# Seven products C by B moved to the transposes of B in a two-layer trunk (Mamba-2 layer, then differential attention)

## The chip, the core and the metric

The kernel runs on one core of one Trainium2 chip. The metric is device microseconds of the whole program, the median of three runs. The core has TensorE (the matmul engine, PE in the profile, with its weight loads shown as PEld), VectorE (DVE), ScalarE (ACT), GpSimd (POOL) and SyncE (SP). Each engine works through its own list of instructions in order and waits at semaphores for the others. Matmuls write to PSUM, eight banks of 128x512 float32; everything else lies in SBUF.

## The reference, cut to what matters

One sequence of 512 tokens of width 1024 goes through a Mamba-2 layer and a differential-attention layer. The change touches the state-space part of the first layer alone. It has eight groups; per group there are B and C (512 tokens x 128 states) and four heads of width 64:

```
cb     = einsum("blgn,bsgn->blsg", c_c, b_c)                            # C by B
y_diag = einsum("blsgr,bsgrp->blgrp", cb[..., None] * decay, x_c)
y_off  = einsum("blgn,bgrpn->blgrp", c_c, state) * exp(acs)[..., None]
new_state = state * exp(acs[:, -1])[..., None, None] + einsum("blgn,blgrp->bgrpn", b_c, x_c * to_end[..., None])
y = gated_group_rms_norm(y + d_skip * xs, z, gate_norm_g)
```

Ahead of it stand an RMS norm, the input projection and a causal convolution of four taps with SiLU; behind it the out projection, added to the residual stream. B and C of a group come out of the convolution.

## The kernel before, in words

**Tiling.** Tokens are cut into four chunks of 128. Large products (input projection, out projection, attention projections) are float32 products made of three matmuls on a high and a low part of each operand (`mm3`, L264). Such a triple over 128 inputs and 512 columns is one unit of the dense stream. The weights arrive from HBM and are split into `whi` (ScalarE) and `wlo` (VectorE).

**Order of the dense stream.** `order_a` (L111) is z0 g0 g1 z1 g2 g3 z2 g4 o0 g5 z3 g6 g7 o1 o2 o3: z is a quarter of the gate projection, g a group's projection to B, C and x, o a quarter of the out projection. Each item has 32 units, o3 has 16 here. `first_layer` (L632) counts units from the start of g0 with `n`. Behind the last unit of an item g, the generator `ssd(g)` (L675) of that group starts.

**What lies between the units.** `ssd(g)` is cut by `yield` into pieces, and `PLACES` (L40) says for each piece and each group how many units behind the end of the group's projection it is put. `resume` (L627) keeps a list `due` of (place, length of the list at that moment); `first_layer` sorts it by these two and, at each unit, issues all pieces whose place has come. The pieces are:

- "cb": four products of C by B into the PSUM bank `pcb` (eight matmul records, since a float32 matmul is two);
- "bt": three transposes of B into `pbt`, copied to `bt` by ScalarE;
- "xt": eight transposes of x into `pxt`; VectorE makes `xdt` and `dx` of them (four instructions), GpSimd makes `xe` of `xdt` (three), and VectorE multiplies `dec`, the decays, by `pcb` (four instructions, L711);
- "st": state products `psA`, `psB` (from `bt` and `xe`) and 64 small products `pyd` (from `dec` and `xdt`); VectorE and GpSimd build the states `hst`;
- "o1", "o2": products `po` of C with the states; then VectorE, GpSimd and ScalarE form gate, squares and the root of the group norm (`y_y`, `y_c`), and ScalarE scales four chunks to `tmp`;
- "y0": eight transposes `pyt` of `tmp`, copied and split to `yh`, `yl` for the out projection.

```
        yield "cb"
        pcb = long_bank(f"pcb{g}")
        for c in range(NQ):
            T.matmul(pcb[:, cs], lhsT=bc[:, cs], rhs=cc[:, cs], start=True, stop=True)
        yield "bt"
        pbt = ss_bank(f"pbt{g}")
        for c in range(3):
            T.transpose(pbt[:, c * P:(c + 1) * P], bc[:, c * P:(c + 1) * P], ident)
```

**What sets the order on each engine.** In this stretch TensorE's instructions keep the order of the program (`T.on`, L785). The order on VectorE, ScalarE and GpSimd is chosen when the program is built, by a planner that runs its own timeline: an engine that is free takes, of the instructions that are ready in that timeline, the one written earliest, and weight splits come with high priority. So `dec` by `pcb` is written in piece "xt" but may stand on VectorE well ahead of `xdt`.

**Buffers.** `pcb` and half of `pyd` share the one bank `long`. B after the convolution has one buffer (the convolution of the next group's B waits for the transposes of this one), C has two, `dec` has two.

Of the kernel before, what the change touches and what calls it, by code (L numbers as in the profile page):

```python
# [37 lines left out]


PLACES = {  # L40
    "cb": (10, 2, 14, 14, 5, 5, 14, 12),
    "bt": (10, 29, 21, 47, 35, 25, 23, 37),
    "xt": (18, 37, 31, 52, 43, 36, 31, 43),
    "st": (29, 47, 39, 63, 53, 47, 39, 53),
# [1240 lines left out]
```

## Time and profile before

| what | value |
|---|---|
| median of three runs | 703.73 us (703.64 to 704.46) |
| profiled execution | 705.32 us, of which the span from first to last instruction is 703.5 us |
| mean granted TensorE clock | 0.998 |
| busy: PE, PEld, DVE, ACT, POOL | 695.2, 580.7, 527.0, 426.3, 115.7 us |
| chain that ended last, share by engine | PE 93%, DVE 2%, ACT 1%, DMA 1% |
| products C by B | 64 records, 8.4 us busy, mean 274 ns |

The times of the profile are microseconds from the start of the span. A timeline row gives the start, the time from the first start to the last end of the merged instructions, engine, line, operation, tiles (out<-in), shape, how many, and in brackets the idle time of the engine before it and what ended it. L74 is the line of a helper, so the tiles' names say which instruction a row is. Matmuls overlap: the distance between two starts tells more of TensorE than the length of one.

### The profile page before, as it was taken

The numbers are of one execution on the slowest core, as the hardware profiler recorded it, in microseconds if no ns is written. First come the engines' busy times: TensorE is split into PE (matmuls) and PEld (weight loads), VectorE is DVE, ScalarE is ACT, GpSimd is POOL, SyncE is SP. The second block draws the span as 40 slices with busy tenths as digits, with TensorE's granted clock in tenths as the row PEclk, the third lists the DMA queues.
The fourth block names the chain that finished last, engine by engine and source line by source line (L and its number), as shares of the span: only waits on it lengthen the run. The fifth ranks groups of instructions, "written<-read, shape, count | busy, mean of one in ns | idle before, by whom it ended". The sixth has DMA issues, their size and how long they took to land.

```text
span 703.5 us, 10459 instructions
## 1 busy us (share of the span) xinstructions
PE 695.2 (99%) x3833; PEld 580.7 (83%) x3833; DVE 527.0 (75%) x1190; ACT 426.3 (61%) x928; POOL 115.7 (16%) x154
## 2 busy tenths in 40 slices
PE   9999999999999999999999999999999999999996
PEld 7888888878888888888888888888888888888884
DVE  6789957799489678568995857467778757787876
ACT  7949474474664637537536258567777667665546
POOL 0025332502415035151211101000000000000002
PEclk9999999999999999999999999999999999999999
DMA  9562404215124313313222112413112221130103
GB/s 340 224 267 85 143 38 165 75 61 180 46 84 170 113 68 120 120 61 120 65 87 90 61 60 68 180 60 120 61 61 96 75 69 61 61 117 4 31 1 119
DMA packets 12627, 70.85 MB, mean 101 GB/s; under 512 B 1568, under 2 KB 2592, under 8 KB 5152
## 3 DMA queue, kind: packets, MB, share of 16 engines
q1 hardware_dynamic: 12288, 69.92, 27.6%
q8 instruction: 30, 0.49, 0.3%
q10 hardware_dynamic: 288, 0.26, 0.1%
q14 instruction: 21, 0.17, 0.1%
HBM read 68.02 MB, written 2.16 MB: 100 GB/s over the span
## 4 chain that ended last, share of the span: by engine, by line
PE 93%; DVE 2%; ACT 1%; issue 1%; DMA 1%; POOL 0%; ACTq 0%; POOLq 0%; SPq 0%
PE pg L74 21%; PE po L74 16%; PE pz L74 13%; PE pt L74 8%; PE pq L74 6%; PE pk L74 6%; PE pv L74 6%; PE pb L74 3%; PE sc L74 3%; PE pyd L74 2%; PE pc L74 2%; PE pyt L74 1%; PE pxt L74 1%; PE psA L74 1%; DMA dec<-acs_d 1%
## 5 line engine op out<-in xcount | busy, mean ns | idle before, releaser
L74 DVE SCALAR_TENSOR_TENSOR wlo<-raw,prm,whi 128x512 fp32r<-128x512 f32 (+1 forms) x236 | 146.8, 674 | 46.9 <-ACT whi L74 46.7
L74 ACT ACTIVATE whi<-raw,prm 128x512 fp32r<-128x512 f32 (+1 forms) x236 | 130.5, 629 | 34.1 <-PE pg L74 8.2
L74 PE MATMUL pg<-a_hi,whi 128*128 128x512 f32 x256 | 102.5, 400 | 0.0
L74 PE MATMUL pg<-a_hi,wlo 128*128 128x512 f32 x256 | 99.9, 390 | 0.0
L74 PE MATMUL pg<-a_lo,whi 128*128 128x512 f32 x256 | 99.7, 390 | 0.0
L74 DVE SCALAR_TENSOR_TENSOR xc<-pg,prc,xc 128x511 f32<-128x511 f32 (+2 forms) x96 | 71.0, 746 | 11.6 <-ACT xc L74 10.4
L74 PEld LDWEIGHTS pg<-a_hi,wlo 128*128 128x128 f32 x256 | 48.1, 188 | 10.2
L74 PEld LDWEIGHTS pg<-a_hi,whi 128*128 128x128 f32 x256 | 48.1, 188 | 9.6
L74 PEld LDWEIGHTS pg<-a_lo,whi 128*128 128x128 f32 x256 | 48.1, 188 | 9.4
L74 PE MATMUL po<-whi,yh 128*128 128x512 f32 x128 | 51.2, 400 | 0.0
L74 PE MATMUL pz<-whi,a_hi 128*128 128x512 f32 (+1 forms) x130 | 49.9, 400 | 0.0
L74 PE MATMUL po<-whi,yl 128*128 128x512 f32 x128 | 49.9, 390 | 0.0
L74 PE MATMUL po<-wlo,yh 128*128 128x512 f32 x128 | 49.9, 389 | 0.0
L74 PE MATMUL pz<-wlo,a_hi 128*128 128x512 f32 (+1 forms) x130 | 48.8, 391 | 0.0
L74 PE MATMUL pz<-whi,a_lo 128*128 128x512 f32 (+1 forms) x130 | 48.7, 390 | 0.0
L1084 POOL TENSOR_TENSOR ot<-x_tok,fg 128x512 f32<-128x512 f32 x4 | 5.0, 1288 | 246.9 <-DVE x_tok L74 246.9
L74 ACT ACTIVATE xc<-xc 128x512 f32<-128x512 f32 x32 | 20.3, 633 | 38.4 <-DVE xc L74 34.5
L74 DVE CUSTOM_DVE_ANT_0 s<-sc,bias 128x128 f32<-128x128 f32 (+3 forms) x64 | 29.4, 488 | 15.9 <-PE sc L74 15.4
L74 ACT ACTIVATE s<-s,mx 128x128 f32<-128x128 f32 (+3 forms) x64 | 35.7, 559 | 9.0 <-DVE mx L74 8.9
L74 ACT ACTIVATE xc<-pg,prc 128x512 f32<-128x512 f32 x32 | 24.8, 776 | 26.5 <-DVE pg L74 25.5
L74 ACT ACTIVATE tmp<-dx 128x256 f32<-128x256 f32 x32 | 13.2, 413 | 45.5 <-DVE dx L74 45.5
L708 POOL TENSOR_TENSOR xe<-xdt,tok 128x256 f32<-128x256 f32 x24 | 14.1, 615 | 162.0 <-DVE xdt L74 162.0
(252 smaller groups left out, 1659.4 us busy)
## 6 DMA issues: line engine op xcount, KB each, us to landing
raw<-in_w_in SPq DMA_DIRECT2D x22, 1024.0 KB, 4.8
raw<-in_w_kvqg SPq DMA_DIRECT2D x16, 1024.0 KB, 4.8
dec<-acs_d SPq DMA_DIRECT2D x8, 1024.0 KB, 5.0
raw<-in_w_out SPq DMA_DIRECT2D x8, 1024.0 KB, 4.8
raw<-in_w_bo SPq DMA_DIRECT2D x4, 1024.0 KB, 4.8
x_tok<-in_x SPq DMA_DIRECT2D x4, 512.0 KB, 9.2
head<-in_first SPq DMA_DIRECT2D x3, 512.0 KB, 6.0
out<-ot SPq DMA_DIRECT2D x6, 256.0 KB, 2.1
```

The source lines that it names most:

```text
L74: i = op(*args, **kw)
L708: GP.tensor_tensor(out=xe[:, c], in0=xdt[:, c], in1=toe_tok[:, c, hs].unsqueeze(2).to_broadcast([P, R, HD]), op=ALU.mult)
L1084: GP.tensor_tensor(out=o, in0=y, in1=f, op=ALU.mult)
```

## The change

Row "cb" of `PLACES` gets the values of row "bt". Nothing else is edited.

```diff
 PLACES = {
-    "cb": (10, 2, 14, 14, 5, 5, 14, 12),
+    "cb": (10, 29, 21, 47, 35, 25, 23, 37),
     "bt": (10, 29, 21, 47, 35, 25, 23, 37),
```

Group 0 keeps its place. For the others, worked out from `order_a`, the places and the sorting of `due`, counted in units from the start of g0:

| group | "cb" before | "cb" after | order on TensorE at the new place |
|---|---|---|---|
| 1 | 66, between o1 and o2 of group 0 | 93 | products, transposes of B |
| 2 | 142 | 149 | y0 of group 1, products, transposes of B |
| 3 | 174, ahead of o1 and o2 of group 2 | 207 | products, y0 of group 2, transposes of B |
| 4 | 229, behind o2 of group 3 | 259 | products, y0 of group 3, transposes of B |
| 5 | 293 | 313 | y0 of group 4, products, transposes of B |
| 6 | 366 | 375 | y0 of group 5, products, transposes of B |
| 7 | 396 | 421 | products, y0 of group 6, transposes of B |

At three of the seven places y0 of the group before comes between the products and the transposes, because a piece that is put on the list anew stands behind one of the same place and number that is there already. At group 2, 5 and 6 y0 is ahead of both.

## Rows read from the trace of the kernel before

**Rows 1.** Page, part 1: busy us, share of the span, records

```profile
PE 695.2 (99%) x3833; PEld 580.7 (83%) x3833; DVE 527.0 (75%) x1190; ACT 426.3 (61%) x928; POOL 115.7 (16%) x154
```

**Rows 2.** Waits of TensorE, whole span: us in total, times, longest

```profile
PE warm L74 <- DVE blank L74: 1.5, 1, 1.5
```

**Rows 3.** Timeline of TensorE at the products of groups 0 and 2

```profile
59.21 1.05 PE L74 MATMUL pcb<-xc,xc 128*128 128x128 f32 x8
60.10 0.49 PE L74 MATMUL pbt<-ident,xc 128*128 128x128 f32 x3
...
142.15 1.05 PE L74 MATMUL pcb<-xc,xc 128*128 128x128 f32 x8
142.95 0.48 PE L74 MATMUL pg<-a_hi,whi 128*128 128x512 f32 x1
143.27 0.40 PE L74 MATMUL pg<-a_lo,whi 128*128 128x512 f32 x1
```

**Rows 4.** Timeline of TensorE at y0 of groups 1 and 5

```profile
147.59 0.39 PE L74 MATMUL pg<-a_hi,wlo 128*128 128x512 f32 x1
148.04 1.96 PE L74 MATMUL pyt<-ident,tmp 128*128 128x128 f32 x8
149.84 0.49 PE L74 MATMUL pbt<-ident,xc 128*128 128x128 f32 x3
...
150.41 0.40 PE L74 MATMUL pg<-a_lo,whi 128*128 128x512 f32 x1
150.64 0.40 PE L74 MATMUL pg<-a_hi,wlo 128*128 128x512 f32 x1
...
334.32 1.03 PE L74 MATMUL pyt<-ident,tmp 128*128 128x128 f32 x8
```

**Rows 5.** Timeline of ScalarE at the scaling of groups 1 and 5

```profile
147.50 1.69 ACT L74 ACTIVATE tmp<-dx,y_y 128x256 f32<-128x256 f32 x4
...
330.99 1.70 ACT L74 ACTIVATE tmp<-dx,y_y 128x256 f32<-128x256 f32 x4
```

**Rows 6.** Timeline of VectorE at the end of group 1's root

```profile
146.78 0.15 DVE L74 SCALAR_TENSOR_TENSOR y_y<-y_c,y_y 128x4 f32<-128x4 f32 x1
146.85 2.47 DVE L74 TENSOR_TENSOR dec<-dec,pcb 128x512 f32<-128x512 f32 x4
```

**Rows 7.** Windows from transposes of B to pyd: length, busy by engine (records), clock, DMA

```profile
149.80:164.20 14.40, 14.40 (x71) 12.10 (x70) 13.48 (x22) 10.43 (x17) 1.76 (x3) 1.00 0.20 74
...
196.30:210.70 14.40, 14.40 (x74) 11.99 (x72) 12.19 (x19) 7.71 (x13) 1.76 (x3) 1.00 0.22 76
...
335.20:348.70 13.50, 13.50 (x67) 11.11 (x65) 12.79 (x20) 9.85 (x17) 1.76 (x3) 1.00 0.22 79
```

**Rows 8.** Timeline of VectorE in group 6, up to xdt

```profile
334.28 2.32 DVE L74 SCALAR_TENSOR_TENSOR xc<-pg,prc,xc 128x511 f32<-128x511 f32 x3 [0.85 <-ACT xc L74]
...
337.83 0.69 DVE L74 TENSOR_TENSOR yl<-pyt,yh 128x512 fp32r<-128x512 f32 x1 [0.64 <-ACT yh L74]
...
343.86 0.69 DVE L74 TENSOR_TENSOR xdt<-pxt,tok 128x512 f32<-128x512 f32 x1
```

**Rows 9.** Timeline of GpSimd at xe of groups 2 and 6

```profile
161.39 1.76 POOL L708 TENSOR_TENSOR xe<-xdt,tok 128x256 f32<-128x256 f32 x3 [24.32 <-DVE xdt L74]
...
345.83 1.76 POOL L708 TENSOR_TENSOR xe<-xdt,tok 128x256 f32<-128x256 f32 x3 [26.03 <-DVE xdt L74]
```

**Rows 10.** Timeline of TensorE at the state products of groups 2 and 6

```profile
163.36 1.02 PE L74 MATMUL psA<-xe,bt 128*128 128x256 f32 x4
...
347.33 1.02 PE L74 MATMUL psA<-xe,bt 128*128 128x256 f32 x4
348.19 0.59 PE L74 MATMUL psB<-xe,bt 128*128 128x256 f32 x2
```

**Rows 11.** Timeline of VectorE at the last state of group 6

```profile
355.51 0.42 DVE L74 TENSOR_TENSOR hst<-psB,hst 128x256 f32<-128x256 f32 x1
```

**Rows 12.** Timeline of TensorE at o1 and o2 of group 6

```profile
356.53 1.46 PE L74 MATMUL po<-hst,xc 128*128 128x256 f32 x6
```

## The prediction, made before the changed kernel was run

> **What bounds the kernel now.** I read the page first, then the waits of TensorE, then the timeline of TensorE around every product C by B and every place that it moves to, and last the lists of ScalarE, VectorE and GpSimd there. The first thing to see is that TensorE is busy for 99% of the span, and that no engine comes near it: VectorE has 75%, ScalarE 61% [rows 1]. The waits name only 1.5 us for TensorE, at the very start [rows 2]. So an instruction that is moved along TensorE's list neither adds nor takes away work; time can change only where TensorE, in its own order, reaches something before its operands are there.
>
> The list of waits does not show all such places, because a wait of TensorE inside a run of transposes is counted as busy. Look at y0 of group 1: eight transposes take 1.96 us, while the same eight take 1.03 in group 5, and they begin 0.45 us behind the start of the dense matmul ahead of them, where two dense matmuls are 0.23 apart [rows 4]. That is 0.93 + 0.22 = 1.15 us of waiting. What they wait for stands on ScalarE: four scalings from 147.50 to 149.19, 0.49 each and 0.40 from one to the next, so the first ends at 147.99 and the first transpose starts at 148.04 [rows 4, 5]. It is the one place between the setup and the last items where I found TensorE over 0.3 us late, and the change touches it.
>
> **The products themselves.** Eight records take from 142.15 to 142.95, 0.80 us, and the dense matmul behind them is followed by the next one after 0.32 instead of 0.23 us [rows 3], so a set of products costs 0.80 + 0.09 = 0.89 us of TensorE. Does it become cheaper next to other float32 work? In group 0 products and transposes stand side by side already, and there the step from the first to the second is 0.89, not 0.80 [rows 3]: the 0.09 is paid between them too. Bounds: nothing saved, and 7 x 0.09 = 0.6 saved if each set lost its changeover; I take 0, by the row of group 0, which is this very pair.
>
> The Trainium skill, "TensorE: Matmul & The Clock Gate", section "Back-to-back issue gap", gives about 81 ns for a matmul of 128 columns in a stream of loads and matmuls. Eight would be 0.65 us, and the sum below would be +1.3 instead of +1.5; the row has 100 ns for each, and the row decides.
>
> **Part 1: y0 of group 1 is reached earlier and waits longer.** Before, the products of group 2 stand at 142.15, ahead of y0; after, they stand behind it. TensorE then comes to y0 0.89 us sooner. Does what it waits for come sooner too? The scalings follow the last step of the root on VectorE, which begins at 146.78; the four products of `dec` by `pcb` stand behind that step, at 146.85 [rows 6], so taking them from this spot frees nothing that the root needs. The root follows the sums of squares and, through them, GpSimd's and VectorE's work on group 1, none of which reads the moved products. So the wait grows from 1.15 by 0.89, and the products are then paid behind it: +0.89 us. Bounds: 0, if the scalings come 0.89 sooner, and 1.5, if the planner puts one 0.69 us product more between two steps of the root (0.60 from start to start, a quarter of 2.40 from rows 6). I take +0.9.
>
> The other six y0: at groups 3, 4 and 7 the products are put ahead of y0 of the group before, so TensorE reaches it no more than 0.4 us sooner (where the transposes of B changed sides with it). At groups 5 and 6 it is reached 0.89 sooner. In group 5's y0, the tighter of the two, the last scaling ends at 332.69 and the first transpose that needs it, three steps of 0.11 behind 334.32, starts at 334.65: 1.96 of slack, 1.07 after [rows 4, 5]. Price 0; without that slack each would cost up to 0.89.
>
> **Part 2: VectorE's four products come later.** They are 2.47 us in one piece, 2.40 as an addition to a full list [rows 6], once per group. Before, they fall soon behind the products, far ahead of `pyd`, which reads them. After, they are not ready before the transposes of B and must be done by `pyd`. What VectorE has free between these two is the question. Group 2 has 14.40 - 13.48 = 0.92, group 3 has 2.21, group 6 has 13.50 - 12.79 = 0.71 [rows 7]. The four groups not shown have more than group 3 and hide the four products, as group 3 does but for 0.2; the cover is this idle time, and if it were gone each would pay as group 6 does.
>
> What stands behind them in the two full stretches is `xdt`, then GpSimd's `xe`, then TensorE's `psA` and `psB`. In group 6 `xdt` starts at 343.86 with no idle time before it, the three `xe` (0.61 apart) end at 346.44, 347.01 and 347.59, and `psA` and `psB` want them at 347.33, 347.76 and 348.19 [rows 8 to 10]. The least slack is 0.60.
>
> How far does `xdt` slip? VectorE has 2.40 us more to do. It gets some back: the convolution products at 334.28 waited 0.85 for ScalarE [rows 8], and ScalarE was free for that at 332.69, when its scalings end [rows 5], so with VectorE's old slot empty they start about 0.85 sooner. The second idle time, 0.64 at 337.83 [rows 8], may be filled too. Slip: 2.40 - 0.85 - 0.64 = 0.9 with both, 1.55 with the first alone. Less the slack: a stall of 0.3 or of 0.95. Below both stands 0, if the planner puts the four products behind `xdt` (they then end near 347.2, ahead of `pyd`, which follows `psB`). Above them 2.40 - 0.60 = 1.8, if nothing is won back. I take 0.6, between the two middle values.
>
> In group 2 the least slack is at `psB` as well: the third `xe` ends at 163.15, and `psB` starts 0.86 behind `psA`'s 163.36, as in group 6, so 1.07 [rows 9, 10]. TensorE comes 0.89 later there, by part 1, so 1.96 against a slip of 2.40 less what is won back: 0. Bound above: 0.4.
>
> The next thing behind is o2 of group 6, whose last pair of matmuls starts 0.86 behind 356.53 and needs a state that VectorE ends at 355.93: slack 1.46 [rows 11, 12]. With the products of group 7 gone from ahead of it, it is reached 0.89 sooner, slack 0.57, and any stall at `psA` widens that again. Price 0; up to 1.2 if VectorE is the full 1.8 behind.
>
> **Sum.** +0.9 + 0.6 = +1.5 us on the profiled execution, 705.32 (span 703.5 and 1.8 around it), so 706.8 there. The median of the three runs shown is 1.59 below that execution; carried over, 703.73 + 1.5 = 705.2.
>
> **Rivals.**
>
> *Part 1 alone.* The planner puts the four products of group 6 behind `xdt`, or wins back more than I think. For it: they are written behind `xdt`. Against: before, the planner let them start ahead of it in every group. +0.9, 704.6.
>
> *VectorE pays in full.* The four products go ahead of `xdt`, nothing is won back, and the root of group 1 gets one more product between its steps: 0.9 + 0.6 + 1.8 = +3.3, 707.0. For it: VectorE's list in group 6 has 0.71 us free [rows 7], and a delay there has no gap to vanish in. Against: the slot that becomes empty is just ahead.
>
> *Not slower: the root of group 1 is planned tighter.* Three products of the next convolution, 2.3 us for such three [rows 8], stand between the last steps of that root before. If the new plan puts them behind the root, the scalings end at about 146.9, ahead of y0 even when TensorE comes sooner; the wait of 1.15 goes with its increase, and with 0.6 in group 6 the sum is -0.6: 703.2, and 702.6 without group 6. It decides at the last step of the root: it must end by about 145.9 instead of 146.93. For it: any edit gives the planner a new timeline. Against: nothing that the root reads is moved, and the convolution products come no later.
>
> *TensorE makes up for it.* If the 99% were less than full work, the dense matmuls behind a wait would close up and a longer wait would cost nothing: 703.7. Rows 4 speak against it: behind the wait of 1.15 us they are 0.23 apart, as ahead of it. The Trainium skill, "Perfetto Trace Analysis", section "Identifying the Most-Contended Engine", says that matmul busy time misleads and that the busy share of weight loads is to be read instead; that is 83% [rows 1], by which a sixth of the span would be room.
>
> **Chances.** My forecast 0.40, part 1 alone 0.26, in full 0.18, tighter root 0.10, made up 0.06. About 0.2%, 1.4 us, is what a measurement of this kernel can tell from no change. The forecast lies just above that bound, with its own range from 704.4 to 706.4, and I give it 0.23 of its 0.40 to the slower side. Slower: 0.23 + 0.18 + 0.05 of part 1 alone = 0.46. Faster: 0.08 of the tighter root, and no more than 0.01 of the rest, 0.09. Within: 0.45. The range for 8 in 10 reaches from 703.0, which leaves out the tighter root without group 6, to 707.4, which leaves out what goes beyond paying in full.
>
> **What would show each step.** Part 1: y0 of group 1 begins to wait at the start of the dense matmul ahead, and from there to its last transpose takes about 0.9 us longer; the last step of the root ends where it did, counted from the `pyd` of group 1. Part 2: a step of more than 0.2 us in TensorE's list ahead of `psA` or `psB` in group 6 and none in group 2, with the four `dec` products between the transposes of B and `xdt`. The others: y0 of groups 2 to 6 at 1.03 us as before. I am wrong if y0 of group 1 waits no longer than before, or if TensorE waits at a place that none of these parts names.

## The result, and the profile after

| | before | after |
|---|---|---|
| median, runs side by side | 703.92 us (703.64 to 704.46, 4 runs) | 707.28 us (707.04 to 709.14, 4 runs) |
| ratio of after to before | | 1.0050, 95% interval 1.0038 to 1.0061 |
| profiled execution, span | 705.32, 703.5 | 709.14, 707.4 |

The change costs 3.36 us, interval 2.7 to 4.3. That is slower, as forecast, but 705.2 was forecast: +3.36 instead of +1.5. It lies near "VectorE pays in full". The profiled execution of after is 1.8 us above the longest of the other three, so shifts between the two traces are larger than the change of the median; they tell where the time goes, and the medians how much.

The page of after, part 1 (busy us, share, records), answers to [rows 1]:

```profile
PE 696.5 (98%) x3833; PEld 579.5 (82%) x3833; DVE 528.4 (75%) x1190; ACT 425.0 (60%) x928; POOL 116.4 (16%) x154
```

The records are the same in number on every engine, and no engine is busier by more than 1.4 us. The work is unchanged; what is added is waiting of TensorE. The waits of TensorE in after (us in total, times, longest) answer to [rows 2], which had the first line alone:

```profile
PE warm L74 <- DVE blank L74: 1.5, 1, 1.5
PE psA L74 <- POOL xe L708: 0.7, 1, 0.7
PE ps_dt L74 <- DVE dtw_raw L74: 0.4, 1, 0.4
PE po L74 <- ACT whi L74: 0.4, 1, 0.4
PE pz L74 <- ACT whi L74: 0.4, 1, 0.4
PE psB L74 <- POOL xe L708: 0.4, 1, 0.4
```

Three of the new lines, `po`, `psA` and `psB`, belong to group 6. The timeline of TensorE there (start, duration, operation; in brackets the idle time before it and its releaser), against [rows 10]:

```profile
334.41 1.03 PE L74 MATMUL pyt<-ident,tmp 128*128 128x128 f32 x8
335.28 1.06 PE L74 MATMUL pcb<-xc,xc 128*128 128x128 f32 x8
336.18 0.49 PE L74 MATMUL pbt<-ident,xc 128*128 128x128 f32 x3
...
346.05 0.39 PE L74 MATMUL po<-whi,yl 128*128 128x512 f32 x1
346.83 0.47 PE L74 MATMUL po<-whi,yh 128*128 128x512 f32 x1 [0.40 <-ACT whi L74]
...
349.89 1.27 PE L74 MATMUL psA<-xe,bt 128*128 128x256 f32 x4 [0.73 <-POOL xe L708]
351.52 0.70 PE L74 MATMUL psB<-xe,bt 128*128 128x256 f32 x2 [0.36 <-POOL xe L708]
```

The products stand directly ahead of the transposes of B, with y0 of group 5 ahead of both, as the text of the change says. Each start can be set against that of the same matmul before. The transposes of B stand at 336.18 against 335.19 (the start of the third window in [rows 7]), 0.99 later. `psA` stands at 349.89 against 347.33, 2.56 later. `psB` is 3.33 later (351.52 against 348.19). So group 6 alone costs 2.34 us between its transposes of B and `psB`. Behind it 0.4 us more is lost, and the dense matmuls behind the last moved products are 3.74 later.

The 0.99 us that TensorE is late at the transposes of B already are for the most part not from y0 of group 1. About 0.5 comes from the setup (last section) and 0.34 from o2 of group 0, with which the products of group 1 have changed places: its six matmuls take 1.80 us from 81.71 on, where 1.46 is usual [rows 12]. The prediction named no wait there. Of the ten profiles with group 1 moved, only the three with a late setup have it (0.34, 0.52 and 0.44).

The list of VectorE in the same stretch, against [rows 8]:

```profile
334.24 2.31 DVE L74 SCALAR_TENSOR_TENSOR xc<-pg,prc,xc 128x511 f32<-128x511 f32 x3 [2.35 <-ACT xc L74]
337.79 1.29 DVE L74 TENSOR_TENSOR yl<-pyt,yh 128x512 fp32r<-128x512 f32 x2 [1.23 <-ACT yh L74]
338.99 2.47 DVE L74 TENSOR_TENSOR dec<-dec,pcb 128x512 f32<-128x512 f32 x4
...
345.94 0.74 DVE L74 SCALAR_TENSOR_TENSOR xc<-pg,prc,xc 128x509 f32<-128x509 f32 x1
346.60 0.68 DVE L74 TENSOR_TENSOR xdt<-pxt,tok 128x512 f32<-128x512 f32 x1
347.20 0.68 DVE L74 TENSOR_TENSOR dx<-pxt,dsk 128x512 f32<-128x512 f32 x1
347.80 0.74 DVE L74 SCALAR_TENSOR_TENSOR xc<-pg,prc,xc 128x511 f32<-128x511 f32 x1
348.46 0.68 DVE L74 TENSOR_TENSOR xdt<-pxt,tok 128x512 f32<-128x512 f32 x1
```

This is the heart of the result. The slot of 2.40 us that the four `dec` products left on VectorE's list stays empty. VectorE now waits 2.35 + 1.23 = 3.58 us for ScalarE ahead of `yl`; before, it waited 0.85 + 0.64 = 1.49 [rows 8]. So 2.09 of the 2.40 became idle time, at places where the moved products are not yet ready (ahead of 334.24) or are queued behind `yl` (ahead of 337.79), and then the full 2.40 comes ahead of `xdt`.

Why the wait grew is read in ScalarE's list of after, against [rows 5]:

```profile
331.85 1.69 ACT L74 ACTIVATE tmp<-dx,y_y 128x256 f32<-128x256 f32 x4
333.45 0.76 ACT L74 ACTIVATE xc<-pg,prc 128x512 f32<-128x512 f32 x1
336.65 0.63 ACT L74 ACTIVATE xc<-xc 128x512 f32<-128x512 f32 x1 [2.44 <-DVE xc L74]
337.19 1.06 ACT L74 CAST yh<-pyt 128x512 fp32r<-128x512 f32 x2
```

VectorE's first convolution product needs ScalarE's first step of the convolution (`xc<-pg,prc`) at 333.45, which follows the four scalings of group 5 (`tmp`). These follow group 5's root. Root and scalings came 0.86 later on the clock (331.85 against 330.99 [rows 5]), while TensorE reached y0 only 0.09 later (334.41 against 334.32 [rows 4]), because the products no longer stood ahead of it. So the products' 0.89 us that TensorE won there was the same 0.85 that VectorE was to win back. And `yh` stands behind a SiLU that itself waits 2.44 for VectorE; before, the first `yh` ran ahead of that SiLU, at 334.95.

GpSimd's three `xe` of group 6, against [rows 9]:

```profile
349.22 2.25 POOL L708 TENSOR_TENSOR xe<-xdt,tok 128x256 f32<-128x256 f32 x3 [28.55 <-DVE xdt L74]
```

At y0 of group 1, where part 1 put its wait, after has (TensorE, against [rows 4]):

```profile
147.70 0.40 PE L74 MATMUL pg<-a_hi,wlo 128*128 128x512 f32 x1
148.20 1.96 PE L74 MATMUL pyt<-ident,tmp 128*128 128x128 f32 x8
150.00 1.06 PE L74 MATMUL pcb<-xc,xc 128*128 128x128 f32 x8
```

The wait is 0.93 + 0.50 - 0.23 = 1.20 us, against 1.15 before. It did not grow by 0.89.

The same windows as [rows 7] of groups 6 and 2, from transposes of B to `pyd`:

```profile
336.20:352.10 15.90, 14.41 (x67) 10.77 (x65) 14.67 (x24) 10.00 (x17) 2.70 (x4) 1.00 0.17 67
150.80:165.20 14.40, 14.40 (x72) 12.12 (x71) 14.34 (x23) 9.03 (x15) 1.76 (x3) 1.00 0.18 73
```

Group 2 is now filled to 14.34 of 14.40 on VectorE, and still TensorE has no wait in it. Group 6's stretch has grown by 2.40, from 13.50 to 15.90.

### The profile page after: what moved, and what is told of

The parts are those of the page before. It is cut to its first block, busy times and chain, and to the rows that moved or that the text cites. A ratio compares the mean times of both kernels' runs of the same rounds, so it can differ in the third digit from the quotient of the medians.

```text
span 707.4 us, 10454 instructions
## 1 busy us (share of the span) xinstructions
PE 696.5 (98%) x3833; PEld 579.5 (82%) x3833; DVE 528.4 (75%) x1190; ACT 425.0 (60%) x928; POOL 116.4 (16%) x154
## 4 chain that ended last, share of the span: by engine, by line
PE 77%; DVE 10%; DMA 4%; ACT 3%; issue 2%; POOL 2%; SPq 0%; ACTq 0%; POOLq 0%; DVEq 0%
PE po L74 15%; PE pg L74 14%; PE pt L74 7%; PE pz L74 7%; PE pq L74 6%; PE pv L74 6%; PE pk L74 6%; DVE wlo L74 3%; PE pb L74 3%; PE sc L74 3%; DVE xc L74 3%; PE pc L74 2%; PE pyd L74 2%; DMA dec<-acs_d 2%; DMA dtw_raw<-in_w_dt 1%
```

## The experiments

Each ratio is against the kernel before, run side by side on the same chip (medians there 704.22, 704.30 and 704.36 us). Each edit is given against the kernel before or the kernel after; where it is one of `PLACES["cb"]`, the line taken out tells which. The changed kernel is at 1.0050 in this measure.

### Which group pays

**Group 6 put back, the other six moved.**

```diff
-    "cb": (10, 29, 21, 47, 35, 25, 23, 37),
+    "cb": (10, 29, 21, 47, 35, 25, 14, 37),
```

> The changed kernel with the products of group 6 alone put back to unit 366. Full-list theory: of the +3.36 us about 2.5 come from group 6, where VectorE's four dec products now stand ahead of xdt in a stretch without idle time, and 0.9 from y0 of group 1. So 704.6 to 705.0 here, no wait of TensorE at psA and psB of group 6, and y0 of group 1 as in the changed kernel. Rival, a share from each of seven groups (the planner's new order everywhere): a seventh goes, 706.8.

Measured: 704.88 us, 1.0008 (1.0000 to 1.0017). Of 3.36 us, 0.66 are left, so group 6 holds about 2.7.

**Group 2 put back, the other six moved.**

```diff
-    "cb": (10, 29, 21, 47, 35, 25, 23, 37),
+    "cb": (10, 29, 14, 47, 35, 25, 23, 37),
```

> The changed kernel with the products of group 2 alone put back to unit 142. Full-list theory: y0 of group 1 waits about as long as before and the 0.9 us go: 706.2 to 706.6, group 6 as in the changed kernel. Rival, a share from each of seven groups: 706.8. Rival, the wait at y0 of group 1 hides a delay that TensorE has anyway: less than 0.4 goes, 706.9 or more.

Measured: 706.98 us, 1.0043 (1.0030 to 1.0057). That is some 0.5 us better than after (0.0007 of 704), between the expectations; the intervals of the two kernels overlap, so this run alone does not show a gain. Group 6 stalls in its profile as in after.

**Group 6 alone moved.**

```diff
-    "cb": (10, 2, 14, 14, 5, 5, 14, 12),
+    "cb": (10, 2, 14, 14, 5, 5, 23, 12),
```

> The kernel before with the products of group 6 alone moved to unit 375. Full-list theory: group 6 by itself costs 2.4 to 2.8 us, since in the run with group 6 put back only 0.66 of the 3.36 was left: ratio to before 1.0034 to 1.0040. Rival, it needs the delays of the earlier moves to be tight there: under 1.5 us, ratio under 1.002.

Measured: 706.64 us, 1.0037 (1.0024 to 1.0049), +2.34 us. Its TensorE has the waits of after, with nothing lost ahead of them:

```profile
347.24 1.27 PE L74 MATMUL psA<-xe,bt 128*128 128x256 f32 x4 [0.73 <-POOL xe L708]
348.87 0.70 PE L74 MATMUL psB<-xe,bt 128*128 128x256 f32 x2 [0.36 <-POOL xe L708]
```

VectorE's list in it has the same idle times too, to the digit, with nothing moved in groups 1 to 5. So the loss comes from group 6's own products and not from what the earlier groups pass on:

```profile
331.60 2.32 DVE L74 SCALAR_TENSOR_TENSOR xc<-pg,prc,xc 128x511 f32<-128x511 f32 x3 [2.35 <-ACT xc L74]
335.15 1.29 DVE L74 TENSOR_TENSOR yl<-pyt,yh 128x512 fp32r<-128x512 f32 x2 [1.23 <-ACT yh L74]
```

**Groups 3, 4, 5 and 7 alone moved.**

```diff
-    "cb": (10, 2, 14, 14, 5, 5, 14, 12),
+    "cb": (10, 2, 14, 47, 35, 25, 14, 37),
```

> The kernel before with the products of groups 3, 4, 5 and 7 moved as in the change; 1, 2 and 6 stay. Full-list theory: VectorE has over 2 us free between the transposes of B and pyd in these four, so nothing is lost: ratio to before 0.9995 to 1.0005. Rival, a share from each moved set: four sevenths of what is left without group 6, 1.0005 or more.

Measured: 704.28 us, 0.9998 (0.9989 to 1.0007). These four cost nothing, as the prediction had it.

**Group 1 alone moved.**

```diff
-    "cb": (10, 2, 14, 14, 5, 5, 14, 12),
+    "cb": (10, 29, 14, 14, 5, 5, 14, 12),
```

> The kernel before with the products of group 1 alone moved to unit 93. o2 of group 0 is reached 0.89 us sooner; in the profiles of three kernels with this move TensorE waits there 0.1 to 0.5 us for the last state. That delays pyd of group 1, from which y0 of group 1 follows, so it stays in the time: ratio 1.0002 to 1.0008. Rival, VectorE had no work but idle time there and the wait is made up at y0 of group 1: 1.000.

Measured: 704.32 us, 0.9998 (0.9989 to 1.0006). No loss: the rival holds.

### Which instruction in group 6

**The four `dec` products of group 6 left out.**

```diff
-        for h in range(R):
+        for h in range(R if g != 6 else 0):
             with ExitStack() if g else tc.issue_after(conv_end[1].ins):
```

> The changed kernel without VectorE's four products of dec by pcb in group 6: the decays of that group are used unmultiplied. TensorE's work and order are the same. Full-list theory: 2.40 us less on VectorE's full list, so group 6 costs nothing: 704.6 to 705.0, the remaining 0.9 at y0 of group 1. Rival, the place of the products on TensorE itself: 707.2. Rival, ScalarE's order (yh of group 5 behind a SiLU that waits 2.4 us for VectorE) costs it: still above 706.

Measured: 705.12 us, 1.0012 (1.0003 to 1.0020), just above the expected range. TensorE's order is that of after, with the transposes of B at 334.95, and it has no wait in group 6:

```profile
347.08 1.02 PE L74 MATMUL psA<-xe,bt 128*128 128x256 f32 x4
347.95 0.59 PE L74 MATMUL psB<-xe,bt 128*128 128x256 f32 x2
```

So it is not the place of TensorE's products that costs but VectorE's work that hangs on them. ScalarE's new order does not cost it by itself either: the idle times of 2.35 and 1.23 us on VectorE are the same as in after. And this run shows how little the rest of VectorE's list comes forward. `xdt` starts here at 343.24, 8.29 behind the transposes of B; before, it was 343.86 - 335.19 = 8.67 [rows 8], with the transposes as above. With no product in the stretch, VectorE is 0.38 us ahead, not 1.49. (What this run still loses is elsewhere: its profile has waits at y0 of group 1 and, in this profile alone, 0.8 us at y0 of group 2, whose eight transposes take 1.86 us.)

```profile
343.24 0.69 DVE L74 TENSOR_TENSOR xdt<-pxt,tok 128x512 f32<-128x512 f32 x1
```

**Two of the four left out.**

```diff
-        for h in range(R):
+        for h in range(R if g != 6 else 2):
             with ExitStack() if g else tc.issue_after(conv_end[1].ins):
```

> The changed kernel with two of the four dec products of group 6 left out (two heads of that group use the decays unmultiplied). Full-list theory: 1.2 us less on VectorE's list; with all four the cost of group 6 is 2.7, with none it is 0.2 to 0.3, so 0.8 to 1.6 with two: ratio 1.002 to 1.0033. Rival, the order that the planner chose and not the length of the list: 1.0043 or, if the order changes, 1.001.

Measured: 705.95 us, 1.0022 (1.0013 to 1.0031). None, two and four products give 705.12, 705.95 and about 707.3: the second pair costs more than the first, as a queue with a little slack does. The trace shows that slack. The transposes of B stand at 335.69 here, and `xdt` starts 9.18 us behind them, 0.51 later than before and so within the slack of 0.60. `psB` starts 13.00 us behind them, exactly as before:

```profile
348.69 0.65 PE L74 MATMUL psB<-xe,bt 128*128 128x256 f32 x2
```

What the run still loses in its profile stands elsewhere, 0.5 us at a tile of o behind `pyd` and 0.44 at o2 of group 0 among it.

**The four products behind `dx`, so behind `xdt`.**

```diff
-                V.tensor_tensor(out=dx[:, :, 2 * j:2 * j + 2, :], in0=pv,
+                dx_end = V.tensor_tensor(out=dx[:, :, 2 * j:2 * j + 2, :], in0=pv,
...
-            with ExitStack() if g else tc.issue_after(conv_end[1].ins):
+            with tc.issue_after(dx_end.ins) if g == 6 else ExitStack() if g else tc.issue_after(conv_end[1].ins):
```

> The changed kernel, TensorE's order untouched, but in group 6 VectorE's four dec products are held behind dx, so xdt goes first. Full-list theory: the waits at psA and psB of group 6 go, 1.5 to 2.5 us of the 3.36; what may remain is a wait at pyd, which needs dec: 704.8 to 705.8. Rival, the place of the products on TensorE itself costs the time: unchanged, 707.2.

Measured: 707.23 us, 1.0047 (1.0035 to 1.0060). Missed, and the most telling miss. The waits at `psA` and `psB` (346.82 and 347.68) are gone, but TensorE now waits a little later, twice, the first time 4 us after its first `pyd` started:

```profile
350.79 0.39 PE L74 MATMUL po<-whi,yl 128*128 128x512 f32 x1
352.31 0.50 PE L74 MATMUL po<-whi,yh 128*128 128x512 f32 x1 [1.13 <-DVE x_tok L74]
...
355.75 0.50 PE L74 MATMUL po<-whi,yh 128*128 128x512 f32 x1 [0.42 <-DVE x_tok L74]
```

The second matmul comes 1.52 us behind the first where 0.23 is usual. It is the first of a tile of o, and waits for the PSUM bank that VectorE frees with `x_tok`. In VectorE's list `x_tok` now stands behind the four products:

```profile
345.28 2.47 DVE L74 TENSOR_TENSOR dec<-dec,pcb 128x512 f32<-128x512 f32 x4
...
351.58 0.68 DVE L74 TENSOR_TENSOR x_tok<-po,x_tok 128x512 f32<-128x512 f32 x1
```

What stands behind the four products on VectorE's list has a TensorE instruction soon behind it, here as in after. This order only changes where the 2.4 us are paid.

### Whether the idle time ahead can be used

**Group 6's products one unit earlier, ahead of y0 of group 5.**

```diff
-    "cb": (10, 29, 21, 47, 35, 25, 23, 37),
+    "cb": (10, 29, 21, 47, 35, 25, 22, 37),
```

> The changed kernel with the products of group 6 at unit 374 instead of 375, so that TensorE does them just ahead of y0 of group 5 and not just behind it. The planner then puts VectorE's four dec products ahead of yl, where VectorE waited 1.23 us for ScalarE. Full-list theory: what counts is how much idle time of VectorE the four products can use, so 1.2 of the 2.7 us of group 6 come back: ratio to before 1.0025 to 1.0033, against 1.0043 to 1.005 for the changed kernel. Rival, only the old slot right behind the root counts: unchanged. Rival, any place ahead of yl will do: 1.0005 to 1.0015.

Measured: 705.22 us, 1.0015 (1.0007 to 1.0024). One unit, the exchange with y0, wins back about 2.4 of the 3.36 us, twice what my theory gave it, and lies at the edge of the rival's range. VectorE's list shows how. The idle time ahead of `yl` is filled, and `yl` no longer waits:

```profile
332.35 2.31 DVE L74 SCALAR_TENSOR_TENSOR xc<-pg,prc,xc 128x511 f32<-128x511 f32 x3 [2.34 <-ACT xc L74]
334.58 2.47 DVE L74 TENSOR_TENSOR dec<-dec,pcb 128x512 f32<-128x512 f32 x4
336.97 1.28 DVE L74 TENSOR_TENSOR yl<-pyt,yh 128x512 fp32r<-128x512 f32 x2
```

The window from the transposes of B to `pyd` (as in [rows 7]) is 13.60 us long, where the same window before, 335.19 to 348.71, has 13.52. VectorE is busy in all of it, with the four products inside, and TensorE loses next to nothing:

```profile
334.18:347.78 13.60, 13.60 (x68) 11.03 (x66) 13.60 (x23) 9.47 (x16) 1.76 (x3) 1.00 0.21 78
```

`xdt` starts 9.20 us behind the transposes, so of the 2.40 us all but 0.53 are hidden, and this is within the slack of 0.60.

**Group 6's products at unit 370, five earlier.**

```diff
-    "cb": (10, 29, 21, 47, 35, 25, 23, 37),
+    "cb": (10, 29, 21, 47, 35, 25, 18, 37),
```

> The changed kernel with the products of group 6 at unit 370, 2.7 us of the dense stream sooner still; the planner puts the four dec products between the first and the second convolution product of C of group 7. Full-list theory: the idle time of 2.35 us ahead of that first product is not reached, since the list is in order, but all behind it is used as at unit 374 or a little better: ratio to before 1.002 to 1.0033. Rival, only the old slot counts: 1.0043 to 1.005. Rival, any place ahead of yl will do: 1.0005 to 1.0015.

Measured: 705.75 us, 1.0021 (1.0012 to 1.0030). Here the four `dec` products stand between the first and the second convolution product, at 333.35, and `yl` does not wait. The 2.35 ahead of the first convolution product stays idle here too. So there is no steady gain with an earlier place: 23, 22, 18 and 14 give 707.3, 705.2, 705.8 and 704.9, and the intervals of the last three overlap.

**`yl` of group 5 behind the four products.**

```diff
-                V.tensor_tensor(out=dec[:, h], in0=dec[:, h], in1=pcb.rearrange("p (c l) -> p c l", l=P), op=ALU.mult)
+                dec_end = V.tensor_tensor(out=dec[:, h], in0=dec[:, h], in1=pcb.rearrange("p (c l) -> p c l", l=P), op=ALU.mult)
+        if g == 6:
+            with tc.issue_after(dec_end.ins):
+                while held:
+                    held.pop(0)()
...
-            V.tensor_tensor(out=yl[:, j, cs], in0=pyt[j][:, cs], in1=yh[:, j, cs].bitcast(F32), op=ALU.subtract)
+            low = lambda j=j, cs=cs: V.tensor_tensor(out=yl[:, j, cs], in0=pyt[j][:, cs], in1=yh[:, j, cs].bitcast(F32), op=ALU.subtract)
+            held.append(low) if g == 5 else low()
```

> The changed kernel, TensorE's order of the pieces untouched; on VectorE the two yl of group 5 stand behind the four dec products of group 6 instead of ahead of them, so that VectorE need not idle 1.23 us for ScalarE's yh while dec is ready. Full-list theory with the idle time in it: 1.2 us of VectorE come back and with them 1.0 to 2.0 us of the 2.7 of group 6: ratio 1.0015 to 1.0033. Rival, the products behind y0 on TensorE cost the time whatever VectorE does: 1.0043 to 1.005.

Measured: 707.77 us, 1.0048 (1.0036 to 1.0061). Missed. The idle time at `yl` is gone just as above, and nothing is won:

```profile
337.49 1.28 DVE L74 TENSOR_TENSOR yl<-pyt,yh 128x512 fp32r<-128x512 f32 x2
...
343.25 0.69 DVE L74 TENSOR_TENSOR pg<-pg,r_row 128x512 f32<-128x512 f32 x1
343.85 1.41 DVE L74 SCALAR_TENSOR_TENSOR wlo<-raw,prm,whi 128x512 fp32r<-128x512 f32 x2
...
345.83 0.68 DVE L74 TENSOR_TENSOR xdt<-pxt,tok 128x512 f32<-128x512 f32 x1
```

Between `yl` and `xdt` the planner put two `wlo` and one `pg` more than in after (6 and 2, against 4 and 1): 2 x 0.66 + 0.60 = 1.92 us. By that sum `xdt` without these would stand 9.15 us behind the transposes of B, as in the run one unit earlier (9.20); with them it stands at 11.07. So the run doesn't speak against the idle time as the cause; it shows that the planner, behind a gap that was filled, can put other work ahead of `xdt` and give the gain away. TensorE waits earlier in this run:

```profile
345.97 0.50 PE L74 MATMUL po<-whi,yh 128*128 128x512 f32 x1 [0.95 <-DVE xc L74]
```

### Part 1 by itself

**The kernel before, with y0 of group 1 three units later.**

```diff
-    "y0": (63, 85, 79, 99, 89, 87, 69, 70),
+    "y0": (63, 88, 79, 99, 89, 87, 69, 70),
```

> The kernel before with y0 of group 1 three units later (152 instead of 149), 2.0 us of the dense stream. If the 1.15 us that TensorE waits there in the profile of before are paid in every execution, this kernel is 1.1 us faster: ratio 0.9984. If that wait comes from a transfer of the decays that was slow in that one execution (the time from pyd of group 1 to the root's end is 27.3 us there and 25.6 to 26.3 in three others with it planned alike), most executions wait little and the gain is under 0.5 us: ratio 0.9993 or more.

Measured: 704.98 us, 1.0012 (1.0003 to 1.0021). No gain, as the second expectation had it, but 0.7 us lost, which neither named. In its profile y0 no longer waits (1.04 us for its transposes), but the transposes of x of group 2, which need a PSUM bank that y0's consumers free, now do:

```profile
155.83 0.60 PE L74 MATMUL pxt<-ident,xc 128*128 128x128 f32 x4
156.78 0.66 PE L74 MATMUL pxt<-ident,xc 128*128 128x128 f32 x4 [0.35 <-DVE yl L74]
```

It also shows that the 1.15 us of [rows 4] were not there to be won. The duration of the eight transposes of y0 of group 1 in the other profiles, with group 2's products ahead of it: 1.15 (group 2 put back), 1.16 (group 6 alone), 1.03 (groups 3, 4, 5, 7), 1.03 (group 1), and 1.96 in the one profile of before. With the products behind it: 1.36, 1.72, 1.73, 1.32, 1.92, 1.53 and 1.71 in the experiments and 1.96 in after. One line of each kind, first of the kernel with group 1 alone moved:

```profile
148.12 1.03 PE L74 MATMUL pyt<-ident,tmp 128*128 128x128 f32 x8
```

The same of the kernel with group 6 put back, where the products of group 2 follow:

```profile
147.45 1.36 PE L74 MATMUL pyt<-ident,tmp 128*128 128x128 f32 x8
```

## Why the prediction was wrong

Two terms of the sum were off. Part 2, the slip of `xdt` in group 6, was put at 0.6 us of waiting and was 2.3: the idle time that was to hide VectorE's work grew instead of being filled. Part 1 was put at 0.9 us and was about 0.6, because its base was a wait of one execution.

**What bounds.** Right. TensorE in its own order is the bound: group 6's 2.34 us of waiting move everything behind them, and the shift grows by 0.4 more, not less, behind them. The rival by which the dense matmuls close up is out. The Trainium skill, "Perfetto Trace Analysis", section "Identifying the Most-Contended Engine", judges the headroom of TensorE by the busy share of the weight loads, besides the share of peak arithmetic, and not by matmul busy time; by that share, a sixth of the span would be left to absorb waits, as an estimate. No run here shows any of it absorbed: at 82% the shift at `psB`, 3.33, is 3.74 behind the last moved products.

**The products themselves, 0.** Right: one set moved (group 1) and four sets moved (3, 4, 5, 7) each gave 0.9998 with at most 0.0009 either way, while the page's records are unchanged.

**Part 1, +0.9.** Right in its place, too large. With group 6 put back 0.66 us are left, with group 2 put back some 0.5 are won, both at the edge of the noise. The seven experiments with the products behind y0 have transposes of 1.61 us on average against the 1.03 of an unhindered set: 0.58. The step that failed is the base: "the wait grows from 1.15 by 0.89". The 1.15 was of that one execution: four profiles of the experiments with the products ahead of y0 have transposes of 1.03 to 1.16 us, and after waits 1.20, hardly longer than before, which the prediction itself gave as a sign of being wrong. (It is also not wholly true that such a wait counts as busy: of the 1.80 us from y0's first transpose to the transposes of B before, 1.58 do.) In its root of group 1, GpSimd reached its copy of the decays at 126.72 after waiting 4.94 us for their transfer; with group 1 alone moved it was 125.58 after 3.33. From the last `pyd` of group 1 to the root's last step the profile of before took 27.28 us; after has 26.59 and the twelve experiments 25.5 to 26.3. So in the other profiles there is next to no such wait, and 0.89 - 0.58 = 0.3 us of the shift goes into slack. Group 1's part is not the rest: it costs nothing alone.

**Part 2, group 6, +0.6.** The mis-sized term, and nearly all of the error: 2.3 to 2.7 us. Where the working failed, step by step in the profile of after:

- "Slip: 2.40 - 0.85 - 0.64 = 0.9 with both, 1.55 with the first alone." `xdt` starts 10.42 us behind the transposes of B, 8.67 before: 1.75. The two idle times gave back 0.65 at most; with the products left out altogether the list comes 0.38 forward. The convolution products did come 0.89 sooner counted from the root (2.96 us behind it instead of 3.85), as I reckoned, but counted from y0 on TensorE only 0.13: TensorE, rid of the products ahead of y0, had moved up by the same amount. I counted that shift at y0 of groups 1, 5 and 6 and not in the cover.
- "The second idle time, 0.64 at 337.83, may be filled too." It grew to 1.23, because `yl` stands ahead of the `dec` products in VectorE's list and waits for ScalarE. One unit earlier, `dec` stands ahead of `yl`, `xdt` slips by 0.53 only, and 2.4 us come back.
- Not in the working: VectorE's list was built anew, and a convolution product went between the first `dx` and the second `xdt` (0.66 from start to start).
- Not in the working: the three `xe` take 2.25 instead of 1.76, 0.49 more.

1.75 + 0.66 + 0.49 = 2.90 is how much later the last `xe` ends, and less the slack of 0.60 that was read right, 2.30: TensorE's `psB` slipped by 2.34. Half a microsecond of that is paid already at 346.83, at the first matmul of a tile of o. The matmul starts 0.15 behind the end of VectorE's last convolution product of B (345.94 + 0.74 = 346.68), and the same tile in the run with `yl` held back names `xc` as its releaser. The profile of after names ScalarE's `whi`, but of the splits there one ends at 346.20 and the next at 346.82, and the matmul's weight load starts at 346.80, between the two. That it waits for the PSUM bank which `xc` reads is argued from these rows, and no run takes it away by itself. It is also a wait at a place that no part of the prediction named.

**"VectorE pays in full" (707.0)** had nearly the right time, in part by luck. For group 6 it is the nearer account (the stall is 1.8 and more), but 0.65 was won back, and the convolution product and the slower `xe` that made up for it are not in it. For the root of group 1 it is wrong: the root got no product more.

**Group 2, 0.** Right: VectorE is full in that stretch, `psA` and `psB` run without a wait. **Groups 3, 4, 5 and 7, 0.** Right. **o2 of group 6, 0.** Right in after: its six matmuls take 1.46 us as before; the 0.3 lost behind `psB` is at a tile of o ahead of it, at 357.94.

What stays open: how much of the planner's new order is a consequence of the place and how much is chance (the run with `yl` held back and the one a unit earlier differ by 2.5 us over two `wlo` and one `pg`), and how the 0.9 us that are left in the version one unit earlier divide: its profile loses 0.3 at y0 of group 1 and 0.4 at two tiles of o behind `pyd`. No version here is faster than the kernel before.

## What to carry to other kernels

When an instruction is moved along the list of the engine that bounds, look for the work that hangs on it on the other engines, and ask whether that work can use the idle time which it leaves: idle time that lies before the work is ready, or ahead of an instruction behind which the work is queued, is not cover. Where the helping engine is 95% full in a stretch (VectorE, 12.79 of 13.50 us), the order on its list decides: with the four products behind a waiting `yl` most of the 2.4 us came out as waits of TensorE, and with them behind `xdt` the waits only moved; with them ahead of `yl`, one unit earlier, all but 0.53 us were hidden and slack took the rest, at 100% busy. And a wait of about a microsecond in a single profile is no base for a sum until a second execution shows it.

## What the runs showed of the hardware that was not expected

- The three `xe` on GpSimd (256 columns each) took 1.76 us in group 6 in most profiles, 2.24 or 2.25 in after and the two others with its order on VectorE, and 2.66 in the run with `yl` held back (start of the first to end of the last). In these four the last of them ran beside VectorE's weight splits `wlo` for 0.58 us and more and took 1.06 or 1.10 us instead of 0.61; in the other ten of group 6 it stood beside them for less than 0.1. The split beside it is slower too. In after the three `xe` last until 351.47, and three splits take 2.78; before, `xe` ended at 347.59, and four take 2.73:

```profile
350.25 2.78 DVE L74 SCALAR_TENSOR_TENSOR wlo<-raw,prm,whi 128x512 fp32r<-128x512 f32 x3
...
347.51 2.73 DVE L74 SCALAR_TENSOR_TENSOR wlo<-raw,prm,whi 128x512 fp32r<-128x512 f32 x4
```

  That the two hinder each other is read from these traces; no run moves the splits by themselves, and in the kernel before one `xe` of group 3 ran beside a single split without delay.
- From one execution to the next the wait of GpSimd for the small transfer of the decays ahead of group 1's root was 4.94 us (before), 4.02 (after) and 2.93 to 3.94 in the experiments. The 1.15 us at y0 of group 1 stand in the profile with the longest of them.
- The setup's `ps_dt` waited 0.42 us for `dtw_raw` in after, 0.2 to 0.3 in two experiments and not in before: it lies ahead of every moved product and is missing in six of the eight experiments that start from the changed kernel, so this half microsecond of the profiled execution of after (709.14, the other three runs 707.04 to 707.35) is not put down to the change.
